# Projecting the indexer's queries for three of four token blocks in a two-layer hybrid attention kernel

## The chip, the core and the metric

The kernel runs on one core of one Trainium2 chip. The metric is the device time of one execution in microseconds (us), the median of several runs. Five engines matter: TensorE (PE in the profile, with PEld for its weight loads), VectorE (DVE), ScalarE (ACT), GpSimd (POOL) and SyncE (SP), which issues most of the DMAs. Each works through its own list of instructions in order.

## The reference

The network has two layers over 512 tokens of 1024 columns. Each layer projects its input x once, into columns that are split between two kinds of attention (group A, stick-breaking; group B, sparse), a small indexer, and gates. Only the indexer is touched by the change:

```python
qA, kA, vA, gA, qB, kB, vB, gB, qI, kI, wI = jnp.split(proj, SPLIT_POINTS, axis=-1)
...
# in dsa_sparse_attention, per block of 128 queries:
rel = jax.nn.relu(jnp.einsum('bqhd,bsd->bqhs', qib, k_idx).astype(jnp.float32))
score = jnp.einsum('bqhs,bqh->bqs', rel, wib.astype(jnp.float32))
chunk_end = (t // CHUNK + 1) * CHUNK
admissible = key_pos[None, :] < chunk_end[:, None]
score = jnp.where(admissible[None], score, -jnp.inf)
vals, idx = lax.top_k(score, topk)
```

The indexer has 8 heads of 64 columns, so qI is 512 columns wide. It scores every key for every query, and each query keeps the best topk = 128 keys that are admissible, that is, that lie in its own chunk of 64 tokens or before it. The queries of the first block, tokens 0 to 127, have at most 128 admissible keys, so they keep all of them whatever their scores are.

## The kernel before

**Layout.** The tokens make four blocks of 128 (tb 0 to 3). The input stands turned, with the 1024 columns on the partitions in eight k chunks (KC), as a high part XH and a rest XL, both in fp32r, [128, 4 blocks, 8 chunks, 128 tokens]. A product in full precision is three matmuls: XH by the weights' high part whi, XL by whi, XH by the weights' low part wlo (`mm3`, lines 254 to 258). Each has up to 512 moving columns, all four blocks at once.

**Units.** The projection is cut into units of 256 columns: ("I", 0, "q") and ("I", 1, "q") are the indexer's queries, below I0 and I1; ("A", 0, "k") and so on are the others. `project_t` (line 260) makes a unit as two column tiles of 128; a tile is eight steps, one for each k chunk, and a step is one `mm3`. A generator yields after each step, so that a planner can mix steps with the attention's own instructions. After a tile's last step its evacuation is queued, and `flush` issues it. `evac_q` (line 339) is the one for queries: two ACT instructions copy the halves of the PSUM tile to fp32r (L342, L343), two DVE instructions make the rests (L344, L345).

**Weights.** The class `Stream` loads weight tiles of 512 KB into two raw buffers by DMAs on SP's queue. A tile is split by ACT (whi, L202) and then by POOL (wlo, L205, two instructions for a tile in the stretches spoken of here). The raw buffer goes to the next DMA once POOL is done. `prep_ahead` issues the split of the tiles that come up next.

**Start of layer 0.** `first_units` (line 363) makes the first unit of values, the indexer's keys and I0 together, chunk by chunk as x and the weights arrive: for each chunk and each of the three products four matmuls into the values and keys (pjv, L405, 328 columns) and two into the two tiles of I0 (pjq, L407, 512 columns). In chunk 0 all pjv come first. In the last chunk (the eighth) the pjq are held back, so that the keys can be evacuated and turned (pk) meanwhile. Layer 1 makes I0 with `project_t`, like any unit, after the values.

**Index slots.** The rest of a layer is a loop over slots s. Slots 0 to 23 are the indexer's tasks, one for a head h = s // 3 and a block qb = 1 + s % 3; block 0 has none, because its queries keep all keys (its mask is the constant of `constants`). In a slot PE makes z, the product of queries with the keys of the blocks up to qb (two matmuls of 256, 384 or 512 columns, L495 and L498); ACT takes it out of PSUM with a relu (L606) and DVE adds it to the block's scores (L614 for head 0, L616 after that). z has four PSUM buffers in turn (two of the pool pz, two of ptr), the relu four SBUF buffers. So z of slot s needs the relu of slot s - 4, and the relu of slot s needs the score of slot s - 4. Slots 0 to 11 read I0, slots 12 to 23 read I1. In layer 0 a few other pieces fall in there: the table of biases (pf on PE, oh on ACT), a subtraction of shifted values on POOL (L831, M<-M) and the value parts (vt) that follow it on ACT and DVE. After slot 23 come the top-k rounds on DVE, and then the attention tasks, 64 slots.

**The order of the work** is set by a planner. `fill` runs steps of the queued units, in the order of `fills()`, until a target is reached; `pins` say how much work shall be done by which slot. A step counted 648 units whatever it was. The first pin is PREFILL = 6 steps ahead of slot 0; the second says that all of I1 (the first unit in the queue) is done by slot 11; the next unit, A0k, is due by slot 24. Between pins the target is a straight line.

Of the kernel before, what the change touches and what calls it, by code (L numbers as in the profile page):

```python
# [14 lines left out]
AF = mybir.ActivationFunctionType  # L15
ALU = mybir.AluOpType

P = 128
D = 1024
S = 512  # L20
DEPTH = 2
KC = D // P
NTB = S // P
# [51 lines left out]
def fills():  # L75

    units = [("I", 1, "q"), ("A", 0, "k"), ("A", 0, "q")]
    units += [("A", 1, "g"), ("A", 1, "k"), ("A", 1, "q"), ("A", 1, "v")]
    units += [("A", 0, "g"), ("B", 0, "g"), ("B", 1, "g"), ("B", 0, "k"), ("B", 0, "q")]
    units += [("B", 0, "v"), ("B", 1, "k"), ("B", 1, "q"), ("B", 1, "v")]  # L80
    return list(zip(units, HEAD_PINS + A_PINS + B_PINS, strict=True))
# [21 lines left out]
def tile_hybrid(ctx: ExitStack, tc: tile.TileContext, xt, x, w_in, w_ki, w_out, ln_g, ln_b, rel_bias, onehot, out, depth=DEPTH):  # L103
    nc = tc.nc
    V, A, G, T = nc.vector, nc.scalar, nc.gpsimd, nc.tensor
# [19 lines left out]
    XH = big.tile([P, NTB, KC, P], F32R, name="XH")  # L125
    XL = big.tile([P, NTB, KC, P], F32R, name="XL")
# [32 lines left out]
    def twin(dst, src):  # L159
        nc.sync.dma_start(dst.bitcast(F32), src.bitcast(F32))  # L160
# [83 lines left out]
    def flush():  # L244
        while later:
            later.pop(0)()
# [4 lines left out]
            stream.prep_ahead()  # L251
        flush()

    def mm3(o, w, kc, first, last):
        o = o.rearrange("p (a b) -> p a b", b=P)
        T.matmul(o, w[0], XH[:, :, kc, :], start=first, stop=False)  # L256
        T.matmul(o, w[0], XL[:, :, kc, :], start=False, stop=False)  # L257
        T.matmul(o, w[1], XH[:, :, kc, :], start=False, stop=last)  # L258

    def project_t(l, unit, evac):  # L260
        for c in range(2):
            w = stream.get(index[l, unit] + c)
            acc = ppj.tile([P, S], F32, tag="pj", name="pj")
            for kc in range(KC):
                mm3(acc, [t[:, kc * P : (kc + 1) * P] for t in w], kc, kc == 0, kc == KC - 1)
                if kc == KC - 1:
                    later.append(lambda c=c, acc=acc: evac(c, acc))
                yield 648

    def project_v(l, unit, vt, keys=None):  # L270
        i = index[l, unit]
# [53 lines left out]
    def run_pending(at_once=False):  # L325
        for p in pending:
            p[0] -= 1
        while pending and (at_once or pending[0][0] < 0):
            pending.pop(0)[1]()
# [6 lines left out]
        for r in range(2):  # L336
            V.tensor_tensor(vv[:, tb, :, HD + HD * r : 2 * HD + HD * r], src[:, :, r, :], hi[r], ALU.subtract)

    def evac_q(tiles, c, p):
        q = qp.tile([P, 2, S], F32R, tag="q", name="q")  # L340
        tiles[c] = q
        A.activation(q[0:64, 0, :], p[0:64], AF.Copy)  # L342
        A.activation(q[64:128, 1, :], p[64:128], AF.Copy)  # L343
        V.tensor_tensor(q[64:128, 0, :], p[0:64], q[0:64, 0, :], ALU.subtract)  # L344
        V.tensor_tensor(q[0:64, 1, :], p[64:128], q[64:128, 1, :], ALU.subtract)  # L345

    def evac_k(tiles, c, p):
        k = kp.tile([P, 4, S], F32R, tag="k", name="k")
        tiles[c] = k
        A.activation(k[0:64, 0, :], p[0:64], AF.Copy)  # L350
        A.activation(k[64:128, 2, :], p[64:128], AF.Copy)
        V.tensor_tensor(k[0:64, 1, :], p[0:64], k[0:64, 0, :], ALU.subtract)
        V.tensor_tensor(k[64:128, 3, :], p[64:128], k[64:128, 2, :], ALU.subtract)
        twin(k[64:128, 0:2, :], k[0:64, 0:2, :])
        twin(k[0:64, 2:4, :], k[64:128, 2:4, :])
# [9 lines left out]
    def first_units(keys, turn_keys, head_weights, evac_qi):  # L365
        unit = [index[0, u] for u in units[:3]]
        q_raw = vp.tile([P, NTB, 4 * P], F32, tag="v", name="q_raw").rearrange("p (c a) b -> p c (a b)", c=2)
        vk_raw = M.rearrange("p a b -> p (a b)")[:, : KC * (W256 + 72)].rearrange("p (a b) -> p a b", b=W256 + 72)
        q_w = [tuple(wp.tile([P, 1024], F32R, tag=tag, name=f"{tag}q{c}") for tag in ("whi", "wlo")) for c in range(2)]
        bias["oh"] = kp.tile([P, 4, S], F32, tag="k", name="oh").rearrange("p a b -> p (a b)")  # L370
        accs = [ppj.tile([P, S], F32, tag="pj", name="pjv") for _ in range(3)]
        q_accs = [pz.tile([P, S], F32, tag="z", name="pjq") for _ in range(2)]
# [28 lines left out]
        def product(j, kc, w, q):  # L401
            x = (XH, XL, XH)[j]
            first, last = kc == 0 and j == 0, kc == KC - 1 and j == 2
            for tb in range(NTB) if q is None else ():
                T.matmul(full[tb], x[:, tb, kc, :], w[j // 2][:, kc % 4, :], start=first, stop=last)  # L405
            for c in q or ():
                T.matmul(q_accs[c].rearrange("p (a b) -> p a b", b=P), q_w[c][j // 2][:, kc * P : (kc + 1) * P], x[:, :, kc, :], start=first, stop=last)  # L407

        for a, b in zip(cuts, cuts[1:]):
            w = joined[a // 4]  # L410
# [24 lines left out]
        for j in range(3):  # L435
            product(j, KC - 1, w, None)
# [80 lines left out]
    nxt = {}  # L517
# [12 lines left out]
    def layer(l):  # L530
        last_layer = l == depth - 1
        st = {}
        QKV = {}
# [20 lines left out]
        def gate(pair, p):  # L554
            assert pair < 4 or not pending
            s = tp.tile([P, S], F32, tag="t", name="sig")
            A.activation(s, p, AF.Sigmoid)
            if ("o", pair, 1) in made:
                V.tensor_tensor(s, p, s, ALU.mult)
                G.tensor_tensor(M[:, pair, :], M[:, pair, :], s, ALU.mult)  # L560
            else:
                assert ("o", pair, 0) not in made
                V.tensor_tensor(M[:, pair, :], p, s, ALU.mult)
            made.add(("g", pair))
# [17 lines left out]
        def project(unit):  # L582
            kind, i, c = unit
            g = (kind, i)
            if c == "v":
                QKV[unit] = vp.tile([P, NTB, 4 * P], F32R, tag="v", name="vt")
                return project_v(l, unit, QKV[unit])
            if c == "g":
                return project_t(l, unit, lambda j, p: gate(2 * GROUPS.index(g) + j, p))
            QKV[unit] = [None, None]  # L590
            evac = evac_q if c == "q" else evac_k
            return project_t(l, unit, lambda j, p: evac(QKV[unit], j, p))


        class Index(Block):
# [181 lines left out]
        queue, total = [], 0  # L777
        pins = [(0, PREFILL * 648)]
        for unit, by in fills():
            total += 16 * 648  # L780
            queue.append(lambda unit=unit: project(unit))
            pins.append((by, total))
        pins.append((P1[0], total))
# [42 lines left out]
        qi = [None, None]  # L826
        QKV["I", 0, "q"] = qi
        if l == 0:
            first_units(nxt["keys"], turn_keys, head_weights, lambda c, p: evac_q(qi, c, p))
            vv = nxt["v"].rearrange("p t (a r) -> p t a r", r=256)  # L830
            pending.append([SHIFT_SLOTS[0], lambda: G.tensor_tensor(V_PREV, V_PREV, V_NOW, ALU.subtract)])  # L831
            for i in range(4):
                pending.append([SHIFT_SLOTS[0] + 4 + i, lambda i=i: value_part(vv, *divmod(i, 2))])
        else:
            gen = project(("I", 0, "q"))
            for step in range(8):
                next(gen)
                flush()
                stream.prep_ahead()
                if step == 1:  # L840
                    turn_keys(nxt["keys"])
            run_pending(at_once=True)
            run(gen)
# [11 lines left out]
        for s in range(SLOTS + 3):  # L855
# [38 lines left out]
            last = s == SLOTS + 2  # L894
# [10 lines left out]
            if s in SPLITS:  # L905
                flush()
                tb = SPLITS.index(s)
# [7 lines left out]
            for h in STORED:  # L915
                if s == AHEAD[h]:
                    by_number[h].load()
                for qb, (by, tb, col) in STORED[h].items():
                    if s == by:
                        n = P * (qb + 1)  # L920
# [106 lines left out]
        if not last_layer:  # L1027
            unit = ("A", 0, "v")
# [64 lines left out]
```

## Time and profile before

| what | value |
|---|---|
| median of three runs | 650.2 us (649.29 to 650.23) |
| span of the profiled execution | 648.1 us, 2.1 us under that median |
| PE, PEld busy | 639.0 us (99%), 550.1 us (85%) |
| DVE, ACT, POOL busy | 491.7, 348.9, 377.5 us |
| L256, L257, L258 (`mm3`) on PE | 177.1, 168.9, 169.6 us |
| index slots of layer 0, 35.5 to 66.0 us | PE 30.50, DVE 25.53, ACT 23.45, POOL 14.27 us busy |
| index slots of layer 1, 355.0 to 385.0 us | PE 30.00, DVE 23.64, ACT 22.83, POOL 12.22 us busy |

Times count from the start of the span. A row of a timeline has the start, the duration, the engine, the line in the kernel before, the operation, out<-in, and in brackets the idle time of the engine just before it and what ended it; xN marks N instructions of one line run together, under the form of the first. A row of a group has the count, then the busy time and the mean in ns, then the idle time before it. A row of waits has the total, how often, and the longest. Matmul durations overlap, because matmuls are pipelined, so the distance of their starts tells their pace. [...]

### The profile page before, as it was taken

The page shows a single profiled execution, that of the slowest core. Times are in us where ns is not written, and L with a number is a line of the kernel's source. Part 1 is how long each engine was busy: PE and PEld are TensorE (multiplying, and loading weights), DVE is VectorE, ACT ScalarE, POOL GpSimd, SP SyncE. Part 2 cuts the span into 40 slices and gives each one's busy share as a digit, 9 for nine tenths or more (in the row PEclk, how much of TensorE's full clock was granted, in tenths as well). Part 3 has the DMA queues.
Part 4 walks back from the last instruction along what each step waited for, and adds up shares of the span by engine and source line. Part 5 has one row for each costly group of instructions (what it writes and reads, how often), then busy time and mean ns, then how long its engine had stood idle before and what let it go on. Part 6 is the DMA issues. An engine that isn't in the chain of part 4 may idle for free.

```text
span 648.1 us, 10438 instructions
## 1 busy us (share of the span) xinstructions
PE 639.0 (99%) x3501; PEld 550.1 (85%) x3501; DVE 491.7 (76%) x1070; ACT 348.9 (54%) x702; POOL 377.5 (58%) x424
## 2 busy tenths in 40 slices
PE   9999999999999999999999999999999999999995
PEld 6988888988889989888898888889888898898885
DVE  3678799989886775667844889999888477666677
ACT  5568454544447476883134764555544566678700
POOL 5443565446766877788233535545576587768721
PEclk9999999999999999999999999999999999999999
DMA  7532425222243475363313252433214424744402
GB/s 226 192 100 77 118 98 131 70 94 99 82 133 94 145 178 172 116 204 116 130 66 115 80 149 82 128 98 97 67 66 147 131 82 135 195 130 133 172 33 98
DMA packets 31781, 77.44 MB, mean 119 GB/s; under 512 B 6572, under 2 KB 10668, under 8 KB 31728
## 3 DMA queue, kind: packets, MB, share of 16 engines
q1 hardware_dynamic: 31440, 76.51, 38.2%
q8 instruction: 28, 0.46, 0.3%
q14 instruction: 25, 0.20, 0.1%
q10 hardware_dynamic: 288, 0.26, 0.1%
HBM read 61.84 MB, written 4.44 MB: 102 GB/s over the span
## 4 chain that ended last, share of the span: by engine, by line
PE 91%; DVE 4%; ACT 2%; POOL 1%; issue 1%; DMA 0%; SPq 0%; DVEq 0%; ACTq 0%; POOLq 0%
PE pj L256 14%; PE pj L258 14%; PE pj L257 14%; PE pjo L771 13%; PE o L665 6%; PE tr L503 5%; PE z L498 4%; PE z L495 4%; PE pjv L287 4%; PE pjv L289 4%; PE pjv L288 4%; PE pjv L405 2%; PE pjq L407 2%; DVE scores L817 1%; DVE m L816 1%; POOL wlo L205 1%
## 5 line engine op out<-in xcount | busy, mean ns | idle before, releaser
L205 POOL TENSOR_TENSOR wlo<-raw,whi 128x256 fp32r<-128x256 f32 (+1 forms) x234 | 222.6, 978 | 122.3 <-ACT whi L202 111.6
L256 PE MATMUL pj<-XH,whi 128*128 128x512 f32 x432 | 177.1, 410 | 0.0
L258 PE MATMUL pj<-XH,wlo 128*128 128x512 f32 x432 | 169.6, 393 | 0.0
L257 PE MATMUL pj<-XL,whi 128*128 128x512 f32 x432 | 168.9, 391 | 0.0
L258 PEld LDWEIGHTS pj<-XH,wlo 128*128 128x128 f32 x432 | 81.1, 188 | 18.5
L256 PEld LDWEIGHTS pj<-XH,whi 128*128 128x128 f32 x432 | 81.4, 188 | 12.3
L257 PEld LDWEIGHTS pj<-XL,whi 128*128 128x128 f32 x432 | 81.7, 189 | 11.3
L202 ACT ACTIVATE whi<-raw 128x1024 fp32r<-128x1024 f32 x78 | 81.9, 1053 | 2.9 <-DMA raw<-in_w_in_dram 2.6
L678 ACT ACTIVATE om<-z 128x128 f32<-128x128 f32 (+1 forms) x64 | 28.0, 438 | 83.5 <-PE z L498 79.6
L684 DVE TENSOR_TENSOR_SCAN om<-om 128x128 f32<-128x128 f32 (+1 forms) x64 | 59.9, 937 | 4.0 <-POOL om L680 3.8
L287 PE MATMUL pjv<-whi,XH 128*128 128x256 f32 x192 | 57.8, 301 | 0.0
L572 POOL TENSOR_TENSOR M<-M,mixt 64x512 f32<-64x512 f32 x22 | 32.8, 1490 | 41.7 <-DVE mixt L571 34.6
L289 PE MATMUL pjv<-wlo,XH 128*128 128x256 f32 x192 | 54.3, 283 | 0.0
L288 PE MATMUL pjv<-whi,XL 128*128 128x256 f32 x192 | 54.1, 282 | 0.0
L816 DVE MAX8 m<-scores 128x8 f32<-128x256 f32 (+2 forms) x96 | 52.8, 550 | 0.1
L817 DVE MATCH_REPLACE8 scores<-m,scores 128x256 f32<-128x256 f32 (+2 forms) x96 | 52.1, 543 | 0.0
L729 ACT ACTIVATE p<-p,mn 128x128 f32<-128x128 f32 (+1 forms) x64 | 35.9, 561 | 23.3 <-DVE mn L724 23.0
L680 POOL TENSOR_SCALAR_AFFINE_SELECT om<-om 128x128 f32<-128x128 f32 x64 | 20.6, 328 | 46.2 <-ACT om L678 39.7
L665 PEld LDWEIGHTS o<-AT,vt 128*128 128x128 f32 x256 | 41.7, 188 | 5.2 <-DVE AT L514 1.0
L665 PE MATMUL o<-AT,vt 128*128 128x512 f32 (+3 forms) x256 | 45.3, 318 | 0.0
L498 PE MATMUL z<-k,q 128*128 128x128 f32 (+3 forms) x128 | 41.6, 325 | 0.0
L771 PE MATMUL pjo<-whi,XH 128*128 128x512 f32 (+1 forms) x118 | 41.2, 388 | 0.0
(160 smaller groups left out, 1342.5 us busy)
## 6 DMA issues: line engine op xcount, KB each, us to landing
raw<-in_w_in_dram SPq DMA_DIRECT2D x66, 512.0 KB, 3.4
k<-k SPq DMA_DIRECT2D x32, 256.0 KB, 6.0
raw<-in_w_out_dram SPq DMA_DIRECT2D x14, 512.0 KB, 3.2
gbias<-f_dram SPq DMA_DIRECT2D x18, 256.0 KB, 5.0
XN<-in_x_dram SPq DMA_DIRECT2D x8, 256.0 KB
y_dram<-XN SPq DMA_DIRECT2D x4, 512.0 KB, 2.7
XN<-y_dram SPq DMA_DIRECT2D x8, 256.0 KB, 3.6
M<-M SPq DMA_DIRECT2D x4, 448.0 KB
```

Of the source, the lines that this page charges most:

```text
L202: A.activation(hi, src, AF.Copy)
L205: low = lambda lo=lo[:, c], src=src[:, c], hi=hi[:, c]: lo_engine.tensor_tensor(lo, src, hi, ALU.subtract)
L256: T.matmul(o, w[0], XH[:, :, kc, :], start=first, stop=False)
L257: T.matmul(o, w[0], XL[:, :, kc, :], start=False, stop=False)
L258: T.matmul(o, w[1], XH[:, :, kc, :], start=False, stop=last)
L287: T.matmul(full, XH[:, tb, kc, :], whi, start=kc == 0, stop=False)
L288: T.matmul(full, XL[:, tb, kc, :], whi, start=False, stop=False)
L289: T.matmul(full, XH[:, tb, kc, :], wlo, start=False, stop=kc == KC - 1)
L498: T.matmul(self.z[:, :nn], c, d, start=False, stop=True)
L665: T.matmul(self.o[:, q0 * P :], vt[:, sb, self.hh * P : (self.hh + 1) * P], at_block(self.at[j], sb, q0, NTB - q0), start=n == 0, stop=n == 7)
L684: V.tensor_tensor_scan(rev, rev, rev, 1.0, ALU.mult, ALU.min)
L771: T.matmul(acc[:, cols], mixed[:, tb, m, :], w[:, cols], start=n == 0, stop=n == len(steps) - 1)
```

## The change

The first block's queries are no longer projected for the indexer. Every matmul, evacuation and planner's cost of I0 and I1 goes over the last three blocks, 384 columns, in both layers: `mm3` and the pjq matmuls of `first_units` take a first block, `evac_q` takes it too, and a step of these two units counts 648 * 3 // 4 = 486 units. The columns of block 0 in the query tiles and in PSUM are left unwritten; nothing reads them. The weights, their loads and their splits stay as they are.

As a step of I1 counts less, and the prefill is still 6 * 648 units, more steps of I1 run ahead of slot 0. Lines after 258 have other numbers in the changed kernel: ACT's and DVE's evacuation is L349 to L352 there, the index product L502 and L505, relu L614, scores L622 and L624.

```diff
-    def mm3(o, w, kc, first, last):
-        o = o.rearrange("p (a b) -> p a b", b=P)
-        T.matmul(o, w[0], XH[:, :, kc, :], start=first, stop=False)
-        T.matmul(o, w[0], XL[:, :, kc, :], start=False, stop=False)
-        T.matmul(o, w[1], XH[:, :, kc, :], start=False, stop=last)
+    def mm3(o, w, kc, first, last, tb):
+        o = o.rearrange("p (a b) -> p a b", b=P)[:, tb:]
+        T.matmul(o, w[0], XH[:, tb:, kc, :], start=first, stop=False)
+        T.matmul(o, w[0], XL[:, tb:, kc, :], start=False, stop=False)
+        T.matmul(o, w[1], XH[:, tb:, kc, :], start=False, stop=last)
+
+    def first_block(unit):
+        return 1 if unit[0] == "I" else 0
+
+    def cost(unit):
+        return 648 * (NTB - first_block(unit)) // NTB
...
-                mm3(acc, [t[:, kc * P : (kc + 1) * P] for t in w], kc, kc == 0, kc == KC - 1)
+                mm3(acc, [t[:, kc * P : (kc + 1) * P] for t in w], kc, kc == 0, kc == KC - 1, first_block(unit))
...
-                yield 648
+                yield cost(unit)
...
-    def evac_q(tiles, c, p):
+    def evac_q(tiles, c, p, tb=0):
...
-        A.activation(q[0:64, 0, :], p[0:64], AF.Copy)
-        A.activation(q[64:128, 1, :], p[64:128], AF.Copy)
-        V.tensor_tensor(q[64:128, 0, :], p[0:64], q[0:64, 0, :], ALU.subtract)
-        V.tensor_tensor(q[0:64, 1, :], p[64:128], q[64:128, 1, :], ALU.subtract)
+        n = slice(tb * P, S)
+        A.activation(q[0:64, 0, n], p[0:64, n], AF.Copy)
+        A.activation(q[64:128, 1, n], p[64:128, n], AF.Copy)
+        V.tensor_tensor(q[64:128, 0, n], p[0:64, n], q[0:64, 0, n], ALU.subtract)
+        V.tensor_tensor(q[0:64, 1, n], p[64:128, n], q[64:128, 1, n], ALU.subtract)
...
-                T.matmul(q_accs[c].rearrange("p (a b) -> p a b", b=P), q_w[c][j // 2][:, kc * P : (kc + 1) * P], x[:, :, kc, :], start=first, stop=last)
+                T.matmul(q_accs[c].rearrange("p (a b) -> p a b", b=P)[:, 1:], q_w[c][j // 2][:, kc * P : (kc + 1) * P], x[:, 1:, kc, :], start=first, stop=last)
...
-            total += 16 * 648
+            total += 16 * cost(unit)
...
-            first_units(nxt["keys"], turn_keys, head_weights, lambda c, p: evac_q(qi, c, p))
+            first_units(nxt["keys"], turn_keys, head_weights, lambda c, p: evac_q(qi, c, p, 1))
```

More of the change, by code (lines that the diff above doesn't have):

```diff
@@ L590, in project @@
             QKV[unit] = [None, None]
-            evac = evac_q if c == "q" else evac_k
-            return project_t(l, unit, lambda j, p: evac(QKV[unit], j, p))
+            if c == "k":
+                return project_t(l, unit, lambda j, p: evac_k(QKV[unit], j, p))
+            return project_t(l, unit, lambda j, p: evac_q(QKV[unit], j, p, first_block(unit)))
         class Index(Block):
```

## The prediction

> **What bounds the kernel now.** I read the page first, for the engines and for the chain that ended last.
>
> ```profile
> span 648.1 us, 10438 instructions
> PE 639.0 (99%) x3501; PEld 550.1 (85%) x3501; DVE 491.7 (76%) x1070; ACT 348.9 (54%) x702; POOL 377.5 (58%) x424
> PE 91%; DVE 4%; ACT 2%; POOL 1%; issue 1%; DMA 0%; SPq 0%; DVEq 0%; ACTq 0%; POOLq 0%
> ```
>
> PE is busy for all but 9 us and carries 91% of the chain. Then the view of waits, for PE alone; these two lines are its whole answer:
>
> ```profile
> PE idle L377 <- DVE warm L374: 1.2, 1, 1.2
> PE pjv L405 <- DVE AT L414: 0.3, 1, 0.3
> ```
>
> PE waits 1.5 us in all, in the first 5 us. So TensorE time taken away is time saved, wherever the next thing PE needs is already there. The question of this case is where it is not. That is read from the timelines of the three places in which the change acts: the start, the index slots of layer 0, and the same in layer 1.
>
> **What one narrower matmul saves.** Rows of PE's timeline around the first index slots of layer 0 (start, duration, instruction):
>
> ```profile
> 31.40 0.40 PE L256 MATMUL pj<-XH,whi 128*128 128x512 f32 x1
> 35.51 0.28 PE L495 MATMUL z<-ki,q 128*128 128x256 f32 x1
> 35.62 0.28 PE L498 MATMUL z<-ki,q 128*128 128x256 f32 x1
> 36.44 0.34 PE L495 MATMUL z<-ki,q 128*128 128x384 f32 x1
> 36.79 0.39 PE L256 MATMUL pj<-XH,whi 128*128 128x512 f32 x1
> ```
>
> Durations overlap, so starts are what count. From 31.40 to 35.51 stand six steps of three 512-column matmuls: 4.11/18 = 0.228 us each. An index product of slot 1 is two matmuls of 384 columns (L495, L498) and takes 36.79 - 36.44 = 0.35, so 0.175 each. One narrowed matmul saves 0.053. There are 48 in each of four projections (I0 and I1 in each layer; two column tiles, eight k chunks, three products): 4 x 48 x 0.053 = 10.2 us, if PE could use all of it.
>
> **Start of layer 0 (I0, 48 matmuls).** Rows of ACT, then of PE:
>
> ```profile
> 7.79 0.48 ACT L156 ACTIVATE AT<-M 128x328 fp32r<-128x328 f32 x1
> 8.80 0.51 ACT L424 ACTIVATE whiq<-q_raw 128x128 fp32r<-128x128 f32 x2 [0.52 <-DMA q_raw<-in_w_in_dram]
> 16.03 0.75 ACT L156 ACTIVATE AT<-M 128x656 fp32r<-128x656 f32 x1 [0.64 <-DMA M<-in_w_ki_dram]
> 8.33 0.87 PE L405 MATMUL pjv<-AT,XH 128*128 128x328 f32 x4
> 9.16 0.73 PE L407 MATMUL pjq<-XH,whiq 128*128 128x512 f32 x2
> 18.23 0.76 PE L405 MATMUL pjv<-AT,XH 128*128 128x328 f32 x4
> ```
>
> The second chunk begins at 8.33, just as ACT has its weights (7.79 + 0.48), and its first pjq pair at 9.16, while ACT makes whiq after a DMA. Here data set the pace: the six matmuls of chunk 0 and one of chunk 1 save nothing. From there 41 remain. The tightest later place is the fifth chunk: needed at 18.23, ready at 16.03 + 0.75 = 16.8, 1.4 us early, and PE arrives there (1 + 4 + 6 + 6) x 0.053 = 0.9 us earlier. Saved: 41 x 0.053 = **2.2 us**.
>
> **Index slots of layer 0 (I1, 48 matmuls, at most 2.5 us).** A step now counts 486 units, so eight steps instead of six run ahead of slot 0 (24 x 0.175 = 4.2 us against 4.1), and eight instead of ten are left for the slots. On PE, at the end of the prefill of layer 0 (whi_371/wlo_372 are the first column tile of I1, whi_378 the second; z is the index product), before:
>
> ```order
> L495 MATMUL z<-ki,q 128x256
> L498 MATMUL z<-ki,q 128x256
> L256 MATMUL pj<-XH,whi_371 128x512
> L257 MATMUL pj<-XL,whi_371 128x512
> L258 MATMUL pj<-XH,wlo_372 128x512
> L495 MATMUL z<-ki,q 128x384
> ```
>
> and now:
>
> ```order
> L256 MATMUL pj<-XH,whi_371 128x384
> L257 MATMUL pj<-XL,whi_371 128x384
> L258 MATMUL pj<-XH,wlo_372 128x384
> L502 MATMUL z<-ki,q 128x256
> L505 MATMUL z<-ki,q 128x256
> L256 MATMUL pj<-XH,whi_378 128x384
> ```
>
> The first tile is finished before slot 0, and so its evacuation and the next weight split move. On ACT, slots 0 to 2 of layer 0 (relu takes z out of PSUM, q<-pj is the evacuation, whi the split of a weight tile of the following unit), before:
>
> ```order
> L606 ACTIVATE relu<-z,absw 128x256
> L202 ACTIVATE whi_470<-raw_376 128x1024
> L606 ACTIVATE relu<-z,absw 128x384
> L606 ACTIVATE relu<-z,absw 128x512
> L342 ACTIVATE q<-pj 64x512
> L343 ACTIVATE q<-pj 64x512
> L202 ACTIVATE whi_504<-raw_383 128x1024
> ```
>
> and now:
>
> ```order
> L614 ACTIVATE relu<-z,absw 128x256
> L349 ACTIVATE q<-pj 64x384
> L350 ACTIVATE q<-pj 64x384
> L202 ACTIVATE whi_482<-raw_376 128x1024
> L202 ACTIVATE whi_489<-raw_383 128x1024
> L614 ACTIVATE relu<-z,absw 128x384
> L614 ACTIVATE relu<-z,absw 128x512
> ```
>
> Evacuation and both splits now stand ahead of the relu of slots 1 and 2. From slot 11 on the order is the old one. What that does is seen from these rows of POOL, DVE, ACT and PE:
>
> ```profile
> 37.44 2.66 POOL L205 TENSOR_TENSOR wlo<-raw,whi 128x512 fp32r<-128x512 f32 x2 [10.13 <-ACT whi L202]
> 41.08 2.74 POOL L205 TENSOR_TENSOR wlo<-raw,whi 128x512 fp32r<-128x512 f32 x2 [0.98 <-ACT whi L202]
> 43.78 2.57 POOL L831 TENSOR_TENSOR M<-M 128x1024 f32<-128x1024 f32 x1
> 42.59 4.18 DVE L616 SCALAR_TENSOR_TENSOR scores<-relu,sgn,scores 128x256 f32<-128x256 f32 x2
> 46.87 0.69 ACT L606 ACTIVATE relu<-z,absw 128x512 f32<-128x512 f32 x1 [2.09 <-DVE scores L616]
> 48.19 0.28 PE L495 MATMUL z<-ki,q 128*128 128x256 f32 x1
> 52.19 1.52 ACT L606 ACTIVATE relu<-z,absw 128x256 f32<-128x256 f32 x3
> 52.93 0.33 PE L495 MATMUL z<-ki,q 128*128 128x384 f32 x1
> L616 DVE SCALAR_TENSOR_TENSOR scores<-relu,sgn,scores 128x256 f32<-128x256 f32 x2 | 0.9, 472 | 0.0
> L616 DVE SCALAR_TENSOR_TENSOR scores<-relu,sgn,scores 128x384 f32<-128x384 f32 x1 | 0.6, 604 | 0.0
> L616 DVE SCALAR_TENSOR_TENSOR scores<-relu,sgn,scores 128x512 f32<-128x512 f32 x2 | 1.5, 738 | 0.0
> L606 ACT ACTIVATE relu<-z,absw 128x512 f32<-128x512 f32 x8 | 5.5, 686 | 2.4 <-DVE scores L616 2.1 <-PE z L498 0.3
> L606 ACT ACTIVATE relu<-z,absw 128x384 f32<-128x384 f32 x8 | 4.6, 577 | 1.2 <-DVE scores L616 1.2
> L342 ACT ACTIVATE q<-pj 64x512 fp32r<-64x512 f32 x2 | 1.2, 584 | 0.0
> ```
>
> POOL works almost without a break from 37.44 to 46.35. While it does, DVE's scores crawl: those of slots 3 and 4 take 42.59 to 46.77 together, 4.18 us, where such scores take 0.47 + 0.60 when POOL is idle (the grouped DVE rows, from 47.3 on). About one score passes each time a POOL instruction ends. ACT's relu of slot 8 waits 2.09 us for the score of slot 4, whose buffer it takes (four relu buffers), and ends at 47.56. PE's z of slot 12, at 48.19, takes the PSUM buffer which that relu frees (four z buffers): 0.6 us to spare.
>
> [...]
>
> Now put the changed order on the same clock, with the prefill's start held at 31.40. ACT evacuates after the relu of slot 0, in 0.95 us (two at 0.58, less 0.11 each, the step from 512 to 384 in the relu rows), and then does both splits end on end. So POOL starts 0.95 later, at 38.4, but loses its gap of 0.98: 38.4 + 2.66 + 2.74 + 2.57 = 46.4, where it ended at 46.35. It is still five instructions, the scores of slots 0 to 4 still leave one by one, and that of slot 4 again ends near 46.8. The relu of slot 8 and the z of slot 12 thus come no earlier than 0.6 before their old places. At slot 16 the room is 52.93 - (52.19 + 0.47) = 0.27, plus 0.22 for the two narrower evacuations that ACT does before: **0.5 us**. The remaining 2 us become PE waiting in slots 5 to 12, which the waits of before don't have. Bounds: 2.5 if this train moves with PE, nothing if it ends half a microsecond later than I think.
>
> **Layer 1, I0 (48 matmuls).** Rows of PE and of what hangs on it on POOL, SP and ACT, with the page's group of weight splits (1053 ns each) and its line of DMA issues (3.4 us is the median time to landing):
>
> ```profile
> 339.52 0.40 PE L256 MATMUL pj<-XH,whi 128*128 128x512 f32 x1
> 350.91 0.39 PE L256 MATMUL pj<-XH,whi 128*128 128x512 f32 x1
> 351.78 2.55 POOL L205 TENSOR_TENSOR wlo<-raw,whi 128x512 fp32r<-128x512 f32 x2 [7.65 <-ACT whi L202]
> 354.36 0.33 SPq L183 DMA_DIRECT2D raw<-in_w_in_dram  x1
> 355.42 0.48 ACT L606 ACTIVATE relu<-z,absw 128x256 f32<-128x256 f32 x1 [2.50 <-PE z L498]
> L202 ACT ACTIVATE whi<-raw 128x1024 fp32r<-128x1024 f32 x78 | 81.9, 1053 | 2.9 <-DMA raw<-in_w_in_dram 2.6
> 360.10 0.40 PE L495 MATMUL z<-ki,q 128*128 128x512 f32 x1
> raw<-in_w_in_dram SPq DMA_DIRECT2D x66, 512.0 KB, 3.4
> ```
>
> From 339.52 to 350.91 PE does this projection without a gap: 48 x 0.053 = **2.5 us**, less 0.2 at most if the low half of I1's second tile, first wanted at 352.9, is not there before its old 353.1. Lower bound 2.3.
>
> **Layer 1, I1 (at most 2.5 us).** The order changes as in layer 0, but POOL has no M<-M here. New is a DMA: the raw weights of the split that now comes early are issued at 354.36, as POOL lets the buffer go (351.78 + 2.55). What leads to it hangs on the evacuation of I0's first tile, which comes 1.3 us earlier, and on ACT's two shorter evacuations; I put the issue at 352.5 and the landing at 355.9. ACT is ready for this split at 355.4 (relu of slot 0 from 352.9 to 353.4, evacuation 0.95, a split 1.05), waits half a microsecond, and reaches the relu of slot 1 at 357.0. PE wants the buffer that this relu frees for slot 5, at 352.5 + 1.6 (five index products) + 2.1 (four steps) = 356.2, and gets it at 357.0 + 0.58 = 357.6: it waits 1.4. Then PE has the narrower steps left and its buffers in time. Gain 2.5 - 1.4 = **1.1**; bounds 0.3 (landing a microsecond later) and 2.5.
>
> **After the index slots** nothing is removed. The chain of waits leaves PE once more, through DVE's evacuation of a query and the top-k rounds, and DVE was idle ahead of it:
>
> ```profile
> 69.62 0.68 DVE L344 TENSOR_TENSOR q<-pj,q 64x512 fp32r<-64x512 f32 x1 [3.11 <-ACT q L343]
> ```
>
> With 3.11 us idle there, that stretch starts when PE lets it and moves along. The narrower evacuations (16 on ACT, 16 on DVE) are counted where they matter, at slot 16; elsewhere they lie beside PE.
>
> **Sum.** 2.2 + 0.5 + 2.5 + 1.1 = 6.3 us, a span of 641.8 instead of 648.1. The median of the runs, 650.2, is 2.1 above the span; I carry that over: **643.9 us**.
>
> **The rivals.**
> - *All of it passes*: POOL's train moves with PE. 185 useful matmuls x 0.053 = 9.8 us, 640.4. For it: PE waits nowhere now. Against it: 0.6 us of room at slot 12 and 0.27 at slot 16. Chance 0.13.
> - *The index slots give nothing or take back*: a DVE score more is held, or the raw weights land late. 2.2 + 2.3 is left, less up to half a microsecond in each layer: 645.2 to 646.4. Chance 0.24.
> - *Weight loads set the pace*: PEld rows have 188 ns for each load; were that the floor, a matmul would save 0.228 - 0.188 = 0.040 and the sum be 41 x 0.040 + 48 x 0.040 + 1.6 = 5.1, 645.1. Against it: 256-column matmuls start 0.11 apart (35.51, 35.62). Chance 0.05. [...]
>
> ```profile
> L256 PEld LDWEIGHTS pj<-XH,whi 128*128 128x128 f32 x432 | 81.4, 188 | 12.3
> ```
>
> - *The change gives nothing that can be measured*, its matmuls being covered in the start and in layer 1 as well: 649.0 to 651.4. PE's missing waits speak against it. Chance 0.04.
> - *Slower*: POOL's closed train lets DVE get no score through at all. Then the scores of slots 0 to 4, up to 0.47 + 0.60 + 0.74 + 0.47 + 0.60 = 2.9 us at the idle rates, begin only at 46.4, and two more are held by the next POOL pair, 1.1. A delay of 4.0 less the 0.5 of room is 3.5 in each layer: 7.0 - 4.7 = 2.3 slower, 652.5. It decides above 2.9 us of delay in a layer. Against it: a score ended 0.4 after each POOL end. Chance 0.04.
>
> **How the numbers follow.** The forecast has 0.50. Its own bounds (0 to 1.0 and 0.3 to 1.6 for the index parts, 0.3 less in the rest) give 642.9 to 645.5; with the second and third rival it is 642.2 to 646.4, which holds 8 in 10. Outside are the full gain, nothing, and slower. 0.2%, 1.3 us, is about what a measurement of this kernel can tell from no change. Faster: 0.50 + 0.13 + 0.24 + 0.05 = 0.92; same 0.04; slower 0.04.
>
> **What would show it.** Right: PE's start of the prefill at 29.2 instead of 31.4; a new PE wait of about 2 us for ACT's relu in slots 5 to 12 of layer 0, with POOL closed from about 36.3 to 44.2; one of about 1.4 at slot 5 of layer 1; starts of 384-column pj matmuls 0.175 apart. Wrong: no PE waits there (full gain), or PE waits after slot 12 as well, or a prefill that starts later than 30.

## The result, and the profile after

The changed kernel takes 644.29 us (median of four runs, 643.86 to 645.48) beside 650.0 for the kernel before on the same chip: a ratio of 0.9918, 95% interval 0.9904 to 0.9932. The forecast was 643.9. The profiled execution was the longest of the four, 645.48 us at a mean granted clock of 0.993; the other three took 643.86 to 644.32 at 0.996 to 0.997. What sets it apart is seen below, and it is kept out of the sum.

From the page of the changed kernel: the span, the busy times, the clock in 40 slices (a digit is tenths of full speed, 9 is 90% or more) and the shares of the chain that ended last.

```profile
span 643.7 us, 10438 instructions
PE 631.1 (98%) x3501; PEld 548.8 (85%) x3501; DVE 493.0 (77%) x1070; ACT 347.1 (54%) x702; POOL 377.9 (59%) x424
PEclk9999999999999999999999899999999999999998
PE 87%; DVE 5%; ACT 2%; issue 2%; POOL 2%; DMA 1%; DVEq 0%; SPq 0%; ACTq 0%; POOLq 0%
```

PE lost 7.9 us of work and its span 4.4. Four points of the chain went from PE to the others. Two slices have a lower clock: the last, where PE has ended, and one in layer 1. The view of waits, for PE (total, times, longest), has one line that is new; the rest is 1.7 us in the first microseconds, 1.5 before:

```profile
PE z L502 <- ACT relu L614: 3.3, 2, 2.0
```

These are two waits for a relu, one in each layer.

**Layer 0.** Timelines of PE, ACT and POOL after the change (start, duration, instruction):

```profile
28.70 0.35 PE L256 MATMUL pj<-XH,whi 128*128 128x384 f32 x1
29.24 0.33 PE L256 MATMUL pj<-XH,whi 128*128 128x384 f32 x1
44.98 0.39 PE L502 MATMUL z<-ki,q 128*128 128x256 f32 x1 [1.35 <-ACT relu L614]
34.69 2.01 ACT L202 ACTIVATE whi<-raw 128x1024 fp32r<-128x1024 f32 x2
44.24 0.69 ACT L614 ACTIVATE relu<-z,absw 128x512 f32<-128x512 f32 x1 [2.09 <-DVE scores L624]
35.83 5.37 POOL L205 TENSOR_TENSOR wlo<-raw,whi 128x512 fp32r<-128x512 f32 x4 [8.00 <-ACT whi L202]
41.15 2.58 POOL L839 TENSOR_TENSOR M<-M 128x1024 f32<-128x1024 f32 x1
```

The prefill begins at 28.70 instead of 31.40. A step of three narrow matmuls takes 29.24 - 28.70 = 0.54, 0.18 each. ACT's two splits stand end on end, POOL works from 35.83 to 43.73 without a gap, the relu of slot 8 waits 2.09 us for a score, and PE's z of slot 12 waits 1.35 us for that relu.

**Layer 1.** PE, ACT, DVE and SP's queue in the same execution:

```profile
349.58 0.28 PE L502 MATMUL z<-ki,q 128*128 128x256 f32 x1
355.48 0.80 PE L502 MATMUL z<-ki,q 128*128 128x512 f32 x1 [2.00 <-ACT relu L614]
350.79 0.47 ACT L614 ACTIVATE relu<-z,absw 128x256 f32<-128x256 f32 x1 [2.19 <-DVE absw L559]
353.77 1.06 ACT L202 ACTIVATE whi<-raw 128x1024 fp32r<-128x1024 f32 x1 [0.55 <-DMA raw<-in_w_in_dram]
354.85 1.52 ACT L614 ACTIVATE relu<-z,absw 128x384 f32<-128x384 f32 x3
344.23 1.23 DVE L319 TENSOR_TENSOR M<-M 128x1024 f32<-128x1024 f32 x1 [0.61 <-DMA M<-M]
350.24 0.33 SPq L183 DMA_DIRECT2D raw<-in_w_in_dram  x1
```

The raw weights of the second split were issued at 350.24 and ACT waited for them until 353.77. PE's second wait, 2.00 us, is at slot 5, where the forecast had one, but longer. The z that ends it takes 0.80 us; behind the same wait in another execution, below, it takes 0.50. The windows view of three stretches around it, and of two at the kernel's end, tells why (stretch, its length, busy time of PE, PEld, DVE, ACT, POOL with counts, granted clock, DMA share, GB/s):

```profile
352.02:355.41 3.39, 1.46 (x9) 1.14 (x7) 2.52 (x3) 2.79 (x5) 2.11 (x2) 1.00 0.27 102
355.43:358.83 3.40, 3.35 (x10) 3.17 (x11) 3.37 (x4) 2.48 (x5) 3.18 (x3) 0.50 0.46 159
358.85:362.20 3.35, 3.35 (x19) 3.11 (x19) 3.35 (x8) 2.47 (x5) 0.00 (x0) 1.00 0.44 157
635.00:638.70 3.70, 1.42 (x12) 1.22 (x11) 3.10 (x9) 0.00 (x0) 0.79 (x1) 1.00 0.38 142
638.75:643.00 4.25, 0.00 (x0) 0.00 (x0) 1.85 (x4) 0.00 (x0) 0.14 (x1) 0.50 0.35 123
```

For 3.4 us from 355.42 TensorE ran at half its clock: PE is busy for all of that stretch with 10 matmuls, against 19 in the next.

### The profile page after: what moved, and what is told of

Same layout as the page of the kernel before. It is cut to its first block, busy times and chain, and to the rows that moved or that the text cites. A ratio compares the mean times of both kernels' runs of the same rounds, so it can differ in the third digit from the quotient of the medians.

```text
span 643.7 us, 10438 instructions
## 1 busy us (share of the span) xinstructions
PE 631.1 (98%) x3501; PEld 548.8 (85%) x3501; DVE 493.0 (77%) x1070; ACT 347.1 (54%) x702; POOL 377.9 (59%) x424
## 4 chain that ended last, share of the span: by engine, by line
PE 87%; DVE 5%; ACT 2%; issue 2%; POOL 2%; DMA 1%; DVEq 0%; SPq 0%; ACTq 0%; POOLq 0%
PE pj L256 13%; PE pjo L779 13%; PE pj L258 13%; PE pj L257 13%; PE o L673 6%; PE tr L510 5%; PE pjv L293 4%; PE z L505 4%; PE pjv L295 4%; PE pjv L294 4%; PE z L502 4%; PE pjv L412 2%; PE pjq L414 1%; DVE scores L825 1%; POOL wlo L205 1%
## 5 line engine op out<-in xcount | busy, mean ns | idle before, releaser
L256 PE MATMUL pj<-XH,whi 128*128 128x512 f32 (+1 forms) x432 | 174.7, 404 | 0.0
L258 PE MATMUL pj<-XH,wlo 128*128 128x512 f32 (+1 forms) x432 | 167.1, 387 | 0.0
L257 PE MATMUL pj<-XL,whi 128*128 128x512 f32 (+1 forms) x432 | 166.4, 385 | 0.0
L256 PEld LDWEIGHTS pj<-XH,whi 128*128 128x128 f32 x432 | 81.7, 189 | 11.2
L505 PE MATMUL z<-k,q 128*128 128x128 f32 (+3 forms) x128 | 41.6, 325 | 0.0
```

What stands on the lines that cost most here:

```text
L256: T.matmul(o, w[0], XH[:, tb:, kc, :], start=first, stop=False)
L257: T.matmul(o, w[0], XL[:, tb:, kc, :], start=False, stop=False)
L258: T.matmul(o, w[1], XH[:, tb:, kc, :], start=False, stop=last)
L505: T.matmul(self.z[:, :nn], c, d, start=False, stop=True)
```

## The experiments

For each kernel, PE's lead over before: the start of an instruction in the profiled execution of before (first row, us) less its start in the kernel's own. "Prefill" and "I0" are the first matmul of these, a slot is its z. Each ratio in the text is against the kernel before on the same chip, whose medians there lie between 649.6 and 650.0 us.

| kernel | median, us | prefill, layer 0 | slot 20 | I0, layer 1 | slot 0 | slot 12 |
|---|---|---|---|---|---|---|
| before, start | 650.0 | 31.40 | 57.77 | 339.52 | 354.99 | 366.79 |
| changed | 644.29 | 2.70 | 2.95 | 2.89 | 5.41 | 4.36 |
| again | 643.95 | 2.52 | 2.74 | 2.70 | 5.22 | 6.08 |
| i0_only | 645.31 | 2.62 | 2.60 | 2.51 | 5.06 | 5.06 |
| i1_only | 648.55 | 0.25 | 0.46 | 0.35 | 0.25 | 1.48 |
| old_order | 641.80 | 2.39 | 4.24 | 4.17 | 7.72 | 8.12 |
| sub_dve | 642.83 | 2.70 | 3.91 | 3.81 | 6.33 | 7.36 |
| early_heads | 643.87 | 2.62 | 2.88 | 2.90 | 5.41 | 6.40 |
| raw_early | 643.83 | 1.98 | 2.23 | 2.13 | 4.65 | 5.41 |
| raw_heads | 643.74 | 2.35 | 2.58 | 2.58 | 5.10 | 6.32 |
| best | 640.52 | 2.29 | 4.89 | 4.83 | 8.39 | 9.28 |
| best_raw | 639.85 | 2.20 | 4.81 | 4.61 | 8.16 | 9.73 |

From slot 12 of layer 1 on the leads stay within 0.25 us to the end of the kernel.

**again**: the changed kernel once more, for a second profile.

> The changed kernel once more, to see whether the half clock of 3.4 us behind PE's 2.2 us gap in layer 1 comes back. If the halving belongs to that gap in every execution: span near 643.7, mean clock 0.993 in all runs. If it depends on the moment: most runs near 642.4 with a mean clock of 0.996 or 0.997, 644.3 us by the median, and a row of half clock only in some profiles.

643.95 us (643.63 to 644.41), ratio 0.9915 (0.9901 to 0.9928). Its waits and the two turning points of layer 1:

```profile
PE z L502 <- ACT relu L614: 2.6, 2, 1.4
```

```profile
349.77 0.28 PE L502 MATMUL z<-ki,q 128*128 128x256 f32 x1
354.90 0.50 PE L502 MATMUL z<-ki,q 128*128 128x512 f32 x1 [1.23 <-ACT relu L614]
353.18 1.06 ACT L202 ACTIVATE whi<-raw 128x1024 fp32r<-128x1024 f32 x1 [0.18 <-DMA raw<-in_w_in_dram]
354.27 2.57 ACT L614 ACTIVATE relu<-z,absw 128x384 f32<-128x384 f32 x5
```

The relu of slot 1 begins 354.27 - 349.77 = 4.50 us after the z of slot 0, where the forecast had 357.0 - 352.5 = 4.5. In the first profile it was 354.85 - 349.58 = 5.27. On the prediction's clock, with layer 0's 2.70 added back, the raw weights are there at 355.88 and the relu begins at 356.97 (forecast 355.9 and 357.0). This execution has no stretch of half clock before the last 6 us, and the index slots of layer 1 gain 6.08 - 5.22 = 0.86 instead of losing 1.05. So the loss belongs to the one execution, and the sum is read from this one: 2.52 + 0.22 + 2.52 + 0.86, less 0.04 between the layers, 6.08 us.

**i0_only** and **i1_only**: one projection narrowed at a time. In the second, the start of layer 0 has its 512 columns back.

```diff
-        return 1 if unit[0] == "I" else 0
+        return 1 if unit == ("I", 0, "q") else 0
```

```diff
-        return 1 if unit[0] == "I" else 0
+        return 1 if unit == ("I", 1, "q") else 0
...
```

> I0 alone is narrowed; I1 is made over all four blocks, with its old cost, so that the order of the index slots is the old one. Theory (I0 saves all that PE does not wait for data, I1 is mostly eaten by the slots): 2.2 to 2.7 in layer 0 and 2.5 in layer 1, 4.7 to 5.2 us faster than before, 644.8 to 645.3. Rival (the slots of layer 1 eat I0's gain too, since the evacuations behind I0 wait for a DMA): 2.5 to 3 faster, about 647.

> I1 alone is narrowed, with its new cost and so the new order of the index slots; I0 is made over all four blocks. Theory: 0.3 to 0.5 in layer 0 and about 1.1 in layer 1, where nothing ahead is moved against its DMA, so 1.3 to 1.6 faster than before, 648.5, with PE waits for ACT's relu at slot 12 of layer 0 and slot 5 of layer 1. Rival (narrower steps save what they save, and the loss of the whole change comes from I0 and I1 together): 5 faster, 645.

I0 alone: 645.31 us (644.77 to 646.87), ratio 0.9937 (0.9925 to 0.9950); PE waits for no z, and the table's leads are flat through both layers' index slots. I1 alone: 648.55 us (648.02 to 650.09), ratio 0.9982 (0.9973 to 0.9991). Both are as expected. The waits for the relu came with it:

```profile
PE z L502 <- ACT relu L614: 2.2, 3, 1.4
```

With 0.21 gained in layer 0 (0.25 to 0.46) and 1.23 in layer 1, I1 brings 1.4 us by the table and 1.1 by the medians, of the 5.1 us of matmuls that it takes away (96 x 0.053); I0 brings 5.1 by the table and 4.3 by the medians, of as much. The waits are I1's.

**old_order**: the change with six narrow steps ahead of slot 0, not eight (`units[3]` is I1, whose step counts 486).

```diff
-        pins = [(0, PREFILL * 648)]
+        pins = [(0, PREFILL * cost(units[3]))]
```

> The whole change, but the prefill counts six narrow steps instead of 6 * 648 units, so ACT's and DVE's order in slots 0 to 2 is the old one and slot 0 begins about 1.0 us earlier. Theory (what holds PE is the train of ACT, POOL and DVE that slot 0 starts, and the moved order starts it late): layer 0 gains about 1.0 to 1.2 more than the changed kernel, layer 1 nothing to 1.5, since PE then waits at slot 7 instead of slot 5: 642.0 to 643.2. Rival (the amount of work on POOL and DVE in these slots sets the pace, in whatever order): the same as the changed kernel, 644.3, with the wait moved.

641.80 us (641.26 to 642.01), ratio 0.9879 (0.9866 to 0.9893): 2.2 us under the changed kernel, a little more than expected. Its ACT, POOL and PE in layer 0:

```profile
32.96 1.05 ACT L202 ACTIVATE whi<-raw 128x1024 fp32r<-128x1024 f32 x1
33.91 1.22 ACT L614 ACTIVATE relu<-z,absw 128x384 f32<-128x384 f32 x2
34.09 2.65 POOL L205 TENSOR_TENSOR wlo<-raw,whi 128x512 fp32r<-128x512 f32 x2 [6.28 <-ACT whi L202]
39.84 2.57 POOL L839 TENSOR_TENSOR M<-M 128x1024 f32<-128x1024 f32 x1
43.66 0.39 PE L502 MATMUL z<-ki,q 128*128 128x256 f32 x1 [0.32 <-ACT relu L614]
```

One split stands ahead of the relu of slots 1 and 2 again. Its prefill begins at 31.40 - 2.39 = 29.01; POOL starts 5.1 us after that (7.1 in the changed kernel) and is through at 42.41 instead of 43.73; the wait at slot 12 is 0.32 instead of 1.35. Layer 0's slots now give 4.24 - 2.39 = 1.85 us. So the two more steps ahead of slot 0 took most of the gain. They act in two ways, which this run undoes together. In the changed kernel the z of slot 0 comes 4.18 us after the prefill's start, here 3.15; and there the evacuation stands ahead of the split, which is the rest of the 2.0 us by which POOL starts later.

**sub_dve**: the change with the subtraction of shifted values on DVE.

```diff
-            pending.append([SHIFT_SLOTS[0], lambda: G.tensor_tensor(V_PREV, V_PREV, V_NOW, ALU.subtract)])
+            pending.append([SHIFT_SLOTS[0], lambda: V.tensor_tensor(V_PREV, V_PREV, V_NOW, ALU.subtract)])
```

> The changed kernel with the values' subtraction of layer 0 (M<-M, 128x1024, 2.58 us on POOL) issued on DVE in place of POOL; nothing is left out. Theory: in layer 0 the z of slot 12 waits 1.35 us because the scores get one slot at each end of POOL's train of four 1.3 us subtractions and this one; with the last taken out of the train the scores run on 2.6 us earlier, DVE pays about 1.2 us for its own subtraction, and the wait goes to under 0.3: 642.6 to 643.2. Rival 1: the amount of work on DVE sets the pace of these slots, so what POOL gives back DVE takes: 643.8 to 644.2 with the wait still over 1 us. Rival 2: the wait goes but comes back later in layer 0, where the vt work met POOL's pair: wait under 0.3, time 643.7 to 644.2.

642.83 us (642.62 to 643.14), ratio 0.9889 (0.9876 to 0.9903): 1.1 us under the changed kernel.

```profile
35.83 5.37 POOL L205 TENSOR_TENSOR wlo<-raw,whi 128x512 fp32r<-128x512 f32 x4 [9.43 <-ACT whi L202]
41.40 1.21 DVE L839 TENSOR_TENSOR M<-M 128x1024 f32<-128x1024 f32 x1
43.24 0.69 ACT L614 ACTIVATE relu<-z,absw 128x512 f32<-128x512 f32 x1 [1.08 <-DVE scores L624]
43.98 0.38 PE L502 MATMUL z<-ki,q 128*128 128x256 f32 x1 [0.36 <-ACT relu L614]
```

POOL is through at 41.20; DVE pays 1.21 us and is still a microsecond ahead, so the relu of slot 8 starts at 43.24 instead of 44.24 and PE's wait falls by 1.0. That POOL's train holds the scores, and they the relu and PE, is shown by taking its last piece away.

**early_heads, raw_early, raw_heads**: layer 1. The first issues the head weights (sgn, absw) at the second step of I0. The second gives one pair of low halves to DVE, after which the raw buffer goes to the next load. The third has both.

```diff
                 if step == 1:
                     turn_keys(nxt["keys"])
+                    head_weights()
...
-        if l:
-            head_weights()
```

```diff
-            run(gen)
+            for _ in gen:
+                flush()
+                stream.prep(stream.want, V)
+            flush()
```

> The changed kernel with the three head-weight instructions of layer 1 (sgn, sgn, absw: 0.47, 0.18 and 0.19 us on DVE) issued at the second step of the first query projection in place of after it; nothing is left out. Theory: the relu of slot 0 no longer waits 2.2 us for absw, ACT's queue behind it (second query evacuation, two weight splits, relu of slot 1) runs up to 2 us earlier until the raw weights' landing holds it, and the PE wait at slot 5 of layer 1 falls from 1.4 to between 0 and 1.0: 643.0 to 643.6, no half clock there. Rival (the landing of the raw weights sets the relu of slot 1 alone, as the prediction had it): the wait at slot 5 stays 1.2 to 1.4 and the time 643.8 to 644.2.

> The changed kernel with one pair of low halves of layer 1 (wlo<-raw,whi, two of 128x512, 2.5 us as a pair on POOL at 347 us) made by DVE in place of POOL; nothing is left out. The raw weights that the relu of slot 1 waits behind are loaded into the buffer that this pair frees. Theory (their landing sets the PE wait at slot 5 of layer 1): DVE makes the pair in about 1.3 us, the load is issued about 1 us earlier, and the wait falls from 1.2 to 1.4 to between 0.2 and 0.8: 643.0 to 643.5. Rival (ACT's queue behind the relu of slot 0 and absw sets it, the landing is only late beside it): wait still 1.0 to 1.4 and the time 643.8 to 644.2.

> The changed kernel with both edits of layer 1 that brought nothing singly (the head weights early, and the pair of low halves on DVE); nothing is left out. Theory (the landing of the raw weights and absw end within half a microsecond of each other, so that the later of the two holds the relu of slot 1 whichever is mended): with both mended PE's wait at slot 5 of layer 1 falls from 1.2 to 1.4 to under 0.7, and the time to 643.0 to 643.5. Rival (something behind both, such as ACT's own work in that queue, is the bound; or the microsecond is given back at slots 5 to 12 to DVE's scores): 643.7 to 644.2.

643.87 (643.63 to 644.24), 643.83 (643.59 to 644.32) and 643.74 us (643.38 to 644.01): each the same as the changed kernel, and each in the range of its rival. ACT in the run with early head weights, then ACT and DVE in that with the pair on DVE:

```profile
350.01 0.47 ACT L614 ACTIVATE relu<-z,absw 128x256 f32<-128x256 f32 x1 [2.00 <-PE z L505]
353.11 1.06 ACT L202 ACTIVATE whi<-raw 128x1024 fp32r<-128x1024 f32 x1 [0.67 <-DMA raw<-in_w_in_dram]
```

```profile
351.24 0.47 ACT L614 ACTIVATE relu<-z,absw 128x256 f32<-128x256 f32 x1 [2.22 <-DVE absw L559]
352.61 2.01 ACT L202 ACTIVATE whi<-raw 128x1024 fp32r<-128x1024 f32 x2
348.04 1.29 DVE L205 TENSOR_TENSOR wlo<-raw,whi 128x512 fp32r<-128x512 f32 x2 [0.18 <-ACT whi L202]
355.27 0.50 PE L502 MATMUL z<-ki,q 128*128 128x512 f32 x1 [1.03 <-ACT relu L614]
```

With absw early, ACT reaches the second split sooner and waits 0.67 us for its weights; PE's wait at slot 5 is 1.35 us, no less than the 1.23 of again. With the weights early, ACT does not wait for them, but absw stands behind the pair on DVE, and 1.03 are left at slot 5. With both mended the wait at slot 5 does fall, and the time does not. PE, ACT and DVE of the third run:

```profile
354.36 0.50 PE L502 MATMUL z<-ki,q 128*128 128x512 f32 x1 [0.57 <-ACT relu L614]
359.21 0.50 PE L502 MATMUL z<-ki,q 128*128 128x512 f32 x1 [0.28 <-ACT relu L614]
353.73 2.68 ACT L614 ACTIVATE relu<-z,absw 128x384 f32<-128x384 f32 x5
358.58 2.80 ACT L614 ACTIVATE relu<-z,absw 128x384 f32<-128x384 f32 x5 [0.96 <-DVE scores L624]
352.84 4.21 DVE L622 TENSOR_SCALAR scores<-relu,sgn 128x256 f32<-128x256 f32 x3
```

What is left at slot 5 is ACT's own queue: the relu of slot 1 starts at 353.73, as the two splits end (351.69 + 2.01). Then three scores take 4.21 us beside POOL's splits, as in layer 0, the relu of slot 7 waits 0.96 us for a score, and the z of slot 11 waits 0.28. The slots gain 6.32 - 5.10 = 1.22 against 0.86, at most 0.4 us for the two. My theory in the third run was half right: two causes end together, but ACT's queue and the scores stand right behind them.

**long_gap** and **mid_gap**: was it the wait that brought the half clock? Two extra copies on ACT, or one, ahead of the relu of slot 1 of layer 1; their result is not used.

```diff
+            if l and s == 1:
+                late = po.tile([P, S], F32, tag="o", name="late")
+                for _ in range(2):
+                    A.activation(late.rearrange("p (a b) -> p a b", b=P), XH[:, :, 0, :], AF.Copy)
             if at(s):
                 tasks[s].stage1()
```

> The changed kernel with two extra ACT copies of 128x512 (about 0.6 us each, their result unused) ahead of the relu of slot 1 in layer 1; nothing else is changed. Both theories have PE's gap at slot 5 of layer 1 grow from 1.4 to about 2.6 us. Theory (a gap of PE of over about 2 us is followed by some 3.4 us at half the granted clock, as in the one profiled execution of the changed kernel that had a gap of 2.2): in the profile a granted clock near 0.5 for about 3.4 us from the gap on, 646.0 to 647.0 us. Rival (the half clock had another cause, or comes only where the gap meets the throttle's own beat): clock stays above 0.95 outside the gap in the profile, 644.9 to 645.3 us.

> The changed kernel with one extra ACT copy of 128x512 (0.6 us, result unused) ahead of the relu of slot 1 in layer 1, in place of the two of the run with the long gap. PE's gap at slot 5 of layer 1 is then about 1.9 to 2.2 us. Theory A (what decides is PE's busy share within one stretch of a fixed beat of 3.41 us, and where the beat lies differs between executions): the executions differ, some at the clock of 0.993 to 0.994 and near 646.0 us, others at 0.996 to 0.998 and near 644.4. Theory B (the length of the gap alone decides, over some 2 us): all executions alike, all near 646.0 at 0.993 to 0.994, or all near 644.4 at 0.996 to 0.998. In the profile the stretch before a half-clock stretch has PE busy for under 1.7 of 3.41 us.

Two copies: 646.57 us (646.34 to 646.71), all five executions at a clock of 0.993 or 0.994. One copy: four executions at 643.96 to 644.41 with 0.996 or 0.997, and one at 646.06 with 0.994. Windows of the two; the edges are chosen a whole number of 3.413 us from the clock's change at the end of each (my estimate of the beat, from the first profile: the two falls of its clock lie 283.3 us apart, 83 times 3.413, and its half clock between them lasts 3.41):

```profile
352.60:356.00 3.40, 0.93 (x6) 0.60 (x4) 1.88 (x2) 2.83 (x5) 2.93 (x3) 1.00 0.03 11
356.02:359.41 3.39, 3.07 (x10) 2.89 (x11) 3.09 (x5) 2.74 (x6) 2.19 (x2) 0.50 0.48 173
```

```profile
351.46:354.86 3.40, 2.45 (x15) 2.08 (x13) 2.53 (x3) 3.09 (x5) 1.68 (x2) 1.00 0.33 128
354.88:358.27 3.39, 2.69 (x14) 2.37 (x15) 2.56 (x3) 3.08 (x7) 3.39 (x3) 1.00 0.44 150
```

PE busy for 0.93 or 1.46 us of a stretch of 3.4: half clock in the next. 2.45: none. With one copy the gap in the profiled execution, 1.67 us, lay across an edge and was shared by two stretches. The five executions of that kernel differ as the theory of a beat has it. Alone they do not rule out a limit on the gap's length, for that differs between executions too (2.00 us in the first profile of the changed kernel, 1.23 in the second). The ends of the kernels tell the two apart, since PE stops there for good. Windows of again, then of sub_dve, with edges on the beat of each:

```profile
633.26:636.66 3.40, 1.54 (x13) 1.33 (x12) 2.80 (x8) 0.00 (x0) 0.38 (x1) 1.00 0.41 154
636.68:640.00 3.32, 0.00 (x0) 0.00 (x0) 2.30 (x5) 0.00 (x0) 0.59 (x1) 0.50 0.29 103
```

```profile
631.91:635.31 3.40, 1.66 (x14) 1.46 (x13) 2.80 (x8) 0.00 (x0) 0.26 (x1) 1.00 0.41 154
635.33:638.72 3.39, 0.00 (x0) 0.00 (x0) 2.42 (x5) 0.00 (x0) 0.71 (x1) 1.00 0.26 96
```

PE's last matmul ends at 634.80 in again and at 633.57 in sub_dve; the clock falls at 636.67 and at 638.73, after 1.9 us of idleness in one and 5.2 in the other. The length of a gap does not give that. PE's busy time in the stretch goes with it in these profiles: 1.54 us is followed by half clock, 1.66 is not, and neither is 1.86 at the end of before:

```profile
638.92:642.33 3.41, 1.86 (x16) 1.66 (x14) 2.81 (x8) 0.00 (x0) 0.06 (x1) 1.00 0.41 154
642.35:645.74 3.39, 0.00 (x0) 0.00 (x0) 2.61 (x5) 0.00 (x0) 0.90 (x1) 1.00 0.21 77
645.77:648.00 2.23, 0.00 (x0) 0.00 (x0) 0.00 (x0) 0.00 (x0) 0.00 (x0) 0.50 0.34 113
```

**best** and **best_raw**: six narrow steps, the subtraction on DVE and early head weights; then the pair on DVE as well.

> The changed kernel with the prefill of six narrow steps (as in the run with the pin scaled by the narrow step), layer 0's values' subtraction on DVE and layer 1's head weights early; nothing is left out. Theory (the waits of 1.0 at slot 12 of layer 0 and of about 0.3 to 1.4 in layer 1 that remain in that run go): 640.2 to 641.2. Rival (these waits are covered there already, PE never stops for them): 641.5 to 642.0, the same as that run.

> The fastest version so far (six narrow prefill steps, layer 0's values' subtraction on DVE, head weights early; 640.52 us) with the same pair of low halves of layer 1 on DVE. Theory (the landing of the raw weights is the 0.5 to 1.0 us that layer 1 still loses between slots 5 and 7): 639.6 to 640.2. Rival (DVE's own queue is late next, since the pair stands in it ahead of the second query subtraction): 640.4 to 640.9.

640.52 us (640.37 to 640.83), ratio 0.9854 (0.9840 to 0.9867), and 639.85 us (639.20 to 639.93), ratio 0.9840 (0.9827 to 0.9854). The waits left in old_order lay otherwise than the first of these expectations has them: 0.32 us at slot 12 of layer 0, 0.96 at slot 7 of layer 1. By the leads, the subtraction brings best 0.75 us over old_order in layer 0, and the early head weights 0.5 in layer 1. In best_raw PE's waits are those of the first microseconds alone:

```profile
PE idle L384 <- DVE warm L381: 1.2, 1, 1.2
PE pjv L412 <- DVE AT L421: 0.2, 1, 0.2
```

With six steps the pair on DVE brings 0.7 us, which with eight brought nothing. Its parts are 2.20 for the start, 2.61 for layer 0's slots (4.81 - 2.20) and 5.12 for layer 1 (9.73 - 4.61): 9.93 us. That is the 9.8 of the rival in which all of it passes. No run has these other edits without the narrowing; that they alone would bring next to nothing is argued from the kernel before, where PE waits for none of what they move.

## Why the prediction was right

- **0.053 us for a matmul.** Right. 48 of them in layer 1's I0 gave 2.51 to 2.55 us (forecast 2.5). The narrow matmuls start 0.174 us apart (23 distances from 28.70 to 32.71), under the 0.188 of a weight load (0.189 in this profile, means of PEld L256), so loads did not set the pace.
- **Start, 2.2.** Right within its spread. Twelve profiled executions with this start begin the prefill at 28.63 to 29.42, 28.95 in the mean, and two with 512 columns at 31.40 and 31.15: 2.3 by the means. The first profile's 2.70 is at the upper end.
- **Layer 0's slots, 0.5.** The mechanism was right to the tenth: shifted by the 2.70 of the start, POOL's train ran from 38.53 to 46.43 (forecast 38.4 and 46.4), and slot 12 gained 3.21 - 2.70 = 0.5. In this profile the scores of slots 0 to 4 end 0.15, 0.21, 0.28, 0.28 and 0.41 us after POOL's five instructions; by what POOL holds them, no view shows. The size was off: another 0.26 was lost from slot 12 to slot 20, so 0.25 remained. The first profile has 0.11 of it in the z of slot 12 and 0.14 in that of slot 16, which starts at 49.88, 0.06 after the relu of slot 12 ends, and whose two matmuls start 0.28 apart instead of 0.18. So slot 16 did hold PE, where the forecast had it; the room of 0.5 that I read there left out these 0.06 and 0.10, and the train was late by the other 0.08. The wait named as about 2 us in slots 5 to 12 was 1.35 at slot 12 by the view. By the starts of PE's rows these slots lose 2.2 us more than before, 1.6 of it at slot 12 and 0.4 at slot 5; modelled matmul ends hide the rest from the view.
- **Layer 1's slots, 1.1.** Near in size: 0.86 in the undisturbed profile (again's), with the wait at slot 5 at 1.23 (forecast 1.4). The relu of slot 1 came when forecast, but the landing of the weights, which the forecast named, held it for 0.18 us only, not half a microsecond, and sending the weights early took 0.2 off the wait. What I did not see: absw holds the relu of slot 0, behind 2.2 us in which ACT is idle, so that ACT reaches the split almost as late as the weights. Two things end there within 0.2 us, and ACT's queue and the scores come next, so mending one, as the prediction's step invites, brings nothing. That the size came out so close is in part luck.
- **Not foreseen: the clock.** The prediction priced PE's new wait at its own length. In the first profiled execution the wait was 0.8 us longer: DVE waited 0.61 us for the copy M<-M, which lies ahead of absw in its list (0.22 in again), and ACT 0.55 for the raw weights (0.18 in again). The half clock that followed cost about 1 us more: PE's lead fell by another 1.0 from slot 5 to slot 7. Together that is the 1.2 to 1.6 us between this execution and the others; its start was 0.2 ahead of again's.
- **Sum.** 6.3 forecast, 6.08 in the undisturbed profile, 5.7 between the medians. That the sum is so close is in part luck as well: in that profile the start gave 0.3 more than forecast and the slots of both layers together 0.5 less.
- **The rivals.** Of the ways to lose the index slots the closed POOL train was the right one in layer 0 (sub_dve and old_order shift it, and PE's wait goes with it). That all passes was not true of this change, but it is of the same narrowing with the work around it put in order. Two numbers of this part do not follow from their own terms: with 2.2 + 2.3 left, less up to 0.5 in each layer, the second rival comes to 645.7 to 646.7, not 645.2 to 646.4, and no rival or bound gives the 642.2 at the range's lower end. Neither changes how the result is read.

## What to carry to other kernels

When PE is the bound and work is taken from it, look at once at what the planner makes of the smaller cost: here the smaller count put two more steps ahead of slot 0, and with them an evacuation and a weight split ahead of two relus, and that took two of the ten microseconds; one line gave them back. Where several producers end together in front of a wait, undo them together before calling any of them innocent. A stall of PE is priced at its length, and here at about 1 us more in the execution where it left PE busy for 1.46 of 3.39 us and half clock followed.

## What was not expected of the hardware

TensorE's granted clock fell to half after a wait of 2.0 us, for 3.41 us (355.42 to 358.83), and then was full again. From that fall to the one at the end of the same execution (between 638.70 and 638.75) it is 283.3 us, 83 times 3.413, which is my estimate of a beat, from these numbers alone. Of the stretches of about 3.4 us laid on it, those with PE busy for 0.93 (long_gap), 1.46 (the first profile) and 1.54 us (again) were followed by half clock; those with 1.66 (sub_dve), 1.86 (before) and 2.45 (mid_gap) were not, as far as modelled matmul ends tell busy time. That a limit lies between 1.54 and 1.66 is an estimate from these six.

The landing of the first loads differs between executions. For the second chunk of x ACT waited 1.12 us, until 7.16, in the profile of before, and 0.50, until 6.25, in that of the changed kernel; for the fifth it waited 1.86 and 2.71. The narrowed start ended at 28.70 in the first profile of the changed kernel and at 29.42 in raw_early. The 0.7 us between them is more than any term of the sum was off in the undisturbed profile.
